# Strassen's scheme for feed-forward blocks 12 to 15 of the opening token group in place of blocks 16 to 19 of the middle group, with the weight sums of four parts made in two lists

## The chip, the core and the metric

The kernel runs on one core of a Trainium2 chip. The core has TensorE (matmuls, PE in the profile, its weight loads PEld), VectorE (DVE), ScalarE (ACT), GpSimd (POOL) and SyncE (SP, which here only issues transfers), and 16 DMA engines. The metric is the device time of one execution in microseconds, the median over several runs.

## What is computed

One layer of a hybrid encoder on 2048 prompt tokens and 64 sample tokens, model width 1024, all in float32: a modulated norm, one input projection, a pooling mixer beside a matrix-memory recurrence, an output projection; then the part that matters here, a gated feed-forward network of hidden width 2816 with a causal convolution of width 3:

```
h2 = rmsnorm(x, g2) * (1 + sc2) + sh2
up = h2 @ w_up                                  # 1024 -> 2 x 2816
conv = b_conv + sum(w_conv[j] * upp[:, j:j + T] for j in range(CONV_W))
a, g = jnp.split(conv, 2, -1)
x = x + gt2 * ((jax.nn.silu(g) * a) @ w_down)   # 2816 -> 1024
```

A final norm follows. The states of the recurrence, of the pool and of the convolution are returned as well.

## The kernel before, in words

**Precision.** Each matmul operand is split into a high and a low part (a ScalarE copy, line 427, and a VectorE subtraction, line 430, for a weight; the like for the moving side), and each product is three matmuls (`PASSES`, line 479). A matmul is 128 x 128 weights by up to 512 columns.

**Groups, blocks and parts.** The feed-forward works on the 2112 tokens in three groups of 704 (`fgroups`; below: opening, middle and last group). The hidden width is 22 blocks of 128. A group takes them in the parts that `PARTS` lists (line 33). In a part each block is first projected up (`Pair.products`, line 1709: Strassen's seven products, 12 matmuls of 352 columns each, so 84 a block; line 1604). Convolution, SiLU, gate and split of a block are spread over the products of the two blocks that follow (`step_2` to `step_7`, `scale_a`, `taps_a`, `gate` and others). The part's blocks are then projected down and added to the residual rows `x3` (`rows_add`, line 2038).

**Two down projections.** A *plain* part (`down`, line 2201) multiplies each block for 8 output rows and two column sections of 448 and 256: 48 matmuls a block, line 2212. A *Strassen* part, for which `paired` (line 38) is true, has four blocks and takes seven products in place of eight (`quad_down`, line 2045): 168 matmuls of 352 columns, line 2073, for the four. It runs one block late: the first block of the next part is projected up first. It needs its gated blocks as sums, made by `step_2` to `step_7` into seven buffers of the tag `av`, and weight sums. At its entry it waits for the last block's two sums from PSUM (`sum_g1`, `sum_a`, line 1613) before more banks are free. Before the change, Strassen parts are the middle group's first five and the last group's first four. The opening group is all plain, in parts of 5, 5, 6 and 6 blocks. The middle group ends with a plain part of two blocks, for which there is code of its own (`nf == 2`).

**Weight sums.** `quad_sums` (line 1654) makes them from `w_quad`, in pieces: a load of 512 KB, four VectorE operations, a store to `dsum` in DRAM. There are two indices `d` to a part and two pieces to an index. Its buffers are of the tag `av` too, which has seven (`AVB`). The weight sums of the up projection (`wsum`) are made earlier; in the opening group all seven units of a block are split, and three of them are stored with their split (`wsplit`), so that the later groups split four.

**Order of the work.** TensorE, ScalarE, VectorE and GpSimd run in the order in which the program is written. Weights come in one stream of units of up to 512 columns (`stream`), loaded by SP up to seven units ahead and split up to four ahead (`pump`, line 437). Work beside the stream is written as generators in the lists `bg[0]` and `bg[1]`. `tick(i)` takes one step of the first one in list `i`: a product has two steps of list 0, a block's products four of list 1, `quad_down` one of list 0 at each half product except that each fourth is one of list 1, `down` one for each row and block unless deferred work (`todo`) is due, of list 1 and 0 in turn. `drain(i)` runs a list to its end at once. List 0 has `quad_sums` in the opening group, and in the others first `final` (line 1915), the last norm of the group before with its stores. List 1 has `prepare` (norm and sums of the next group's inputs, stored to `Bd`), and in the last part `reload` (the seven inputs brought back as `hx`).

**The end of a group.** Before the last part is projected down, both lists are drained and `reload` is listed. After a plain part of six blocks, each finished row is squared by ScalarE and added up by GpSimd (`fsq_acc`, line 2028) as it ends. After the part of two blocks, `final` does this at the beginning of the next group, with VectorE for the additions (line 2034), and only six of the inputs are reloaded in the part, the seventh at the end.

Of the kernel before, what the change touches and what calls it, by code (L numbers as in the profile page):

```python
# [29 lines left out]
EB = 1  # L30
AVB = 7
ENDS = ((0, 448), (448, 704))
PARTS = (((0, 5), (5, 10), (10, 16), (16, 22)), ((0, 4), (4, 8), (8, 12), (12, 16), (16, 20), (20, 22)),
         ((0, 4), (4, 8), (8, 12), (12, 16), (16, 22)))
NQ, QUADS = 4, 5


def paired(g, part):
    return g > 0 and part[1] - part[0] == NQ
EPS = 1e-6  # L40
HD = 128
NH = 4
# [23 lines left out]
def tile_layer(ctx: ExitStack, tc: tile.TileContext, xT, vecs, cst, rst, w_mod, w_ada, w_qkou, w_v, w_pool,  # L66
# [38 lines left out]
    bg = ([], [], [], [], [])  # L105

    def tick(i=0):
        q = bg[i]
        while q:
            try:  # L110
                next(q[0])
                return
            except StopIteration:
                q.pop(0)

    def drain(*which):
        for i in which or (0, 1, 2, 3, 4):
            while bg[i]:
                tick(i)
# [153 lines left out]
    for g in range(NG):  # L273
        o = Grp()
# [83 lines left out]
    for g in range(NFG):  # L358
        held = None
        late = []  # L360
        for (f0, f1_) in PARTS[g]:
            for f in range(f0, f1_):
# [12 lines left out]
            for i, (n, k) in enumerate(order):  # L375
# [3 lines left out]
                if k % 4 == 0 or (n, c) not in seen:  # L379
                    seen.add((n, c))  # L380
                    d = min(c + 4, f1_)
# [287 lines left out]
    for g in range(NFG):  # L669
        o = Grp()  # L670
# [980 lines left out]

        act.activation(to.t[:, :FH], bk.t[:, :FH], AF.Copy)  # L1652

    def quad_sums():

        for d in range(2 * QUADS):
            for c in (0, 256):
                t = f2.tile([P, 2, FT], F32R, tag="av", name="qs", bufs=AVB)
                w = t.bitcast(F32).rearrange("p a t -> p (a t)")[:, :1024].rearrange("p (i c) -> p i c", i=4)
                nc.sync.dma_start(out=w, in_=w_quad[d, :, :, c:c + 256])  # L1660
                for _ in range(5):
                    yield
                a11, a12, a21, a22 = (w[:, i] for i in range(4))
                dve.tensor_tensor(out=a22, in0=a21, in1=a22, op=ALU.add)
                yield
                dve.tensor_tensor(out=a21, in0=a11, in1=a21, op=ALU.subtract)
                yield
                dve.tensor_tensor(out=a11, in0=a22, in1=a11, op=ALU.subtract)
                yield
                dve.tensor_tensor(out=a12, in0=a12, in1=a11, op=ALU.subtract)  # L1670
                yield
                yield
                nc.sync.dma_start(out=dsum[d, :, :, c:c + 256], in_=w)
                yield
                yield
                yield

# [20 lines left out]
    class Pair:  # L1698
# [3 lines left out]
        quad = d = None  # L1702
# [189 lines left out]
    def reload(Bo, names):  # L1892
        for nm in names:
            Bo.load(nm)
            yield
            yield

    def load_x2(o, ks=range(KD)):
        x3 = []
        for k in ks:  # L1900
            x = f2.tile([P, FT], F32, tag=f"x{k}", name=f"x{k}")
            nc.sync.dma_start(out=x, in_=x2d[k, :, o.t0:o.t0 + FT])
            x3.append(x)
        return x3
# [247 lines left out]
    for o in fgroups:  # L2152
        Bo = B[o.g]
        held = None
        for pi, part in enumerate(PARTS[o.g]):
            f0, f1_ = part
            nf = f1_ - f0
            lastp = pi == len(PARTS[o.g]) - 1
            ends = o.last and lastp
            av = [None] * nf  # L2160
            quad = Quad() if paired(o.g, part) else None
            if pi == 0:
                pair = None
            for f in range(f0, f1_):
                old, pair = pair, Pair(o, Bo, f, f - f0, av, quad)
                pair.products(old)
                if o.g == 0 and len(x3) < KD or pi == 0 and not bg[0]:
                    x3 += load_x2(o, range(len(x3), min(len(x3) + 2, KD)))
                if held is not None and nf > 2:
                    quad_down(o, held, pair, old)  # L2170
                    held = None
            if pi == 0 and o.g > 0:
                drain(0)
                x3 += load_x2(o, range(len(x3), KD))
            if not o.last:
                if pi == 0:
                    if o.g == 0:
                        bg[0].append(quad_sums())
                    bg[1].append(prepare(fgroups[o.g + 1], fscr))
                if lastp:  # L2180
                    drain(0, 1)
                    if nf == 2:
                        for p in (old, pair):
                            p.d = f1.tile([P, 2, HX], F32R, tag="hx", name="av", bufs=2 * len(BN))
                    B.append(Sums())
                    bg[1].append(reload(B[-1], ("B11", "T1", "T2", "B21", "B22", "T3") if nf == 2 else BN))
# [89 lines left out]
            pair = None  # L2276
        if not o.last:
            drain(1)
            if nf == 2:
                Bn = B[-1]  # L2280
                Bn.load(BN[-1])
            bg[0].append(final(o, x3, ssum, nf == 2))
            x3 = []
# [87 lines left out]
```

## Time and profile before

| | |
|---|---|
| median of three runs | 2170.43 us (2169.34 to 2173.03) |
| the profiled execution | 2169.81 us |
| its span, first to last instruction | 2168.0 us |
| granted TensorE clock, mean | 0.998 |
| VectorE, ScalarE, GpSimd busy | 77%, 51%, 12% |
| HBM read, written | 414.65 MB, 128.08 MB |
| DMA, mean rate over the span | 252 GB/s |

How to read the profile: busy rows give line, engine, operation, names (out<-in), shape and count, then busy us, mean ns of one, and the engine's idle time before them. The chain of work that ended last gives start and length in us of each piece. The timeline merges neighbours on one engine; a number in square brackets is idle time, with what ended it. Matmuls are pipelined, so the mean of one (over 300 ns) is longer than the distance from one start to the next, which is the pitch. Tables by stretch give the stretch, its length, busy time and count of each engine, the granted clock, the DMA engines' busy share and GB/s. By time, the feed-forward begins near 787 us; the middle group begins at 1251.6 us and the last at 1701.3 us.

### The profile page before, as it was taken

What the parts mean: (1) busy time and instruction counts of PE and PEld (TensorE: products, weight loads), DVE (VectorE), ACT (ScalarE), POOL (GpSimd) and SP (SyncE); (2) the same over time, 40 slices, a digit from 0 to 9 for tenths busy, and PEclk for the clock granted to TensorE, in tenths of its full rate; (3) what the DMA queues carried; (4) which work ended last, traced back from release to release, by engine and by line L of the source; (5) the groups of instructions that cost most, each with busy time, mean ns of one, the idle gap of its engine ahead of it and who ended that gap; (6) DMA issues with size and microseconds to landing.
All of it is one profiled execution on the core that took longest, in us unless ns stands there. A gap on an engine that the chain in (4) does not pass through costs nothing.

```text
span 2168.0 us, 38128 instructions
## 1 busy us (share of the span) xinstructions
PE 2146.5 (99%) x13529; PEld 2040.9 (94%) x13529; DVE 1666.4 (77%) x3107; ACT 1104.1 (51%) x2201; POOL 249.3 (12%) x468
## 2 busy tenths in 40 slices
PE   8999999999999999999999999999999999999998
PEld 7888888888899999999999999999999999999998
DVE  5777678677675878797968668988888797887874
ACT  4554335334333556464736445655656455565554
POOL 0010000001000301010101220100101121111112
PEclk9999999999999999999999999999999999999999
DMA  8987997897788686888968976666666875555542
GB/s 317 330 307 228 321 317 252 282 320 269 246 286 281 229 268 232 293 288 301 353 235 307 319 264 206 226 227 200 219 232 230 277 269 190 171 175 188 173 157 76
DMA packets 302439, 545.28 MB, mean 252 GB/s; under 512 B 25984, under 2 KB 118656, under 8 KB 302248
## 3 DMA queue, kind: packets, MB, share of 16 engines
q1 hardware_dynamic: 291656, 517.64, 70.6%
q10 hardware_dynamic: 10592, 25.20, 3.0%
q8 instruction: 107, 1.75, 0.3%
q14 instruction: 84, 0.69, 0.1%
HBM read 414.65 MB, written 128.08 MB: 250 GB/s over the span
## 4 chain that ended last, share of the span: by engine, by line
PE 60%; DVE 3%; DMA 1%; issue 1%; ACT 1%; POOL 0%; SPq 0%; DVEq 0%; POOLq 0%; ACTq 0%
PE mm L1604 37%; PE mm L2212 11%; PE mm L2073 10%; PE mm L494 2%; DVE wt L430 1%; DVE tg L1582 0%; ACT tg L1577 0%; DMA wt<-dsum 0%; DMA wt<-wsum 0%; DMA fscr<-h2d 0%; DVE ea L1613 0%; DVE eg L1613 0%; DVE x L2042 0%; DVE tg L1809 0%; ACT mm L1652 0%
## 5 line engine op out<-in xcount | busy, mean ns | idle before, releaser
L1604 PE MATMUL mm<-hx,wt 128*128 128x352 f32 x5544 | 887.1, 321 | 0.9 <-DVE wt L430 0.7
L1604 PEld LDWEIGHTS mm<-hx,wt 128*128 128x128 f32 x5544 | 880.5, 188 | 2.2 <-DVE wt L430 1.9
L494 PE MATMUL mm<-hl,wt 128*128 128x512 f32 (+2 forms) x1920 | 385.8, 356 | 0.3 <-DMA wt<-hl_kept 0.3
L427 ACT ACTIVATE wt<-raw 128x512 fp32r<-128x512 f32 (+3 forms) x468 | 275.9, 597 | 191.0 <-PE mm L494 53.4
L430 DVE TENSOR_TENSOR wt<-raw,wt 128x512 fp32r<-128x512 f32 (+3 forms) x468 | 307.3, 663 | 74.8 <-ACT wt L427 73.3
L494 PEld LDWEIGHTS mm<-hl,wt 128*128 128x128 f32 x1920 | 314.7, 188 | 48.1 <-issue 4.4
L2073 PE MATMUL mm<-av,wt 128*128 128x352 f32 x1512 | 248.2, 324 | 2.7 <-DVE ea L1613 1.2
L2073 PEld LDWEIGHTS mm<-av,wt 128*128 128x128 f32 x1512 | 242.3, 188 | 6.2 <-DVE ea L1613 4.0
L2042 DVE SCALAR_TENSOR_TENSOR x<-mm,MOD,x 128x352 f32<-128x352 f32 (+5 forms) x384 | 180.3, 508 | 69.0 <-PE mm L2212 54.1
L2212 PE MATMUL mm<-av,wt 128*128 128x448 f32 (+1 forms) x1440 | 232.2, 322 | 0.0
L2212 PEld LDWEIGHTS mm<-av,wt 128*128 128x128 f32 x1440 | 221.2, 188 | 9.9
L1652 ACT ACTIVATE mm<-mm 128x352 f32<-128x352 f32 x204 | 91.4, 448 | 235.9 <-PE mm L1604 176.6
L494 PE MATMUL mm<-mx,wt 128*128 128x512 f32 (+1 forms) x960 | 182.2, 351 | 1.2 <-DVE scr L266 1.2
L494 PEld LDWEIGHTS mm<-mx,wt 128*128 128x128 f32 x960 | 158.5, 188 | 24.1 <-DVE scr L266 1.1
L1582 DVE SCALAR_TENSOR_TENSOR ta<-ea,V,ta 128x704 f32<-128x704 f32 (+1 forms) x132 | 125.6, 952 | 54.8 <-ACT ta L1577 48.2
L1582 DVE SCALAR_TENSOR_TENSOR tg<-eg,V,tg 128x704 f32<-128x704 f32 (+1 forms) x132 | 125.7, 952 | 50.5 <-ACT tg L1577 48.0
L430 DVE TENSOR_TENSOR wt<-wt 128x512 fp32r<-128x512 f32 x204 | 138.4, 683 | 11.6 <-ACT wt L427 11.6
L427 ACT ACTIVATE wt<-wt 128x512 fp32r<-128x512 f32 x204 | 123.6, 622 | 34.0 <-DMA wt<-wsum 31.0
L1560 POOL COPY ea<-UC 128x2 f32<-128x2 f32 x66 | 32.7, 496 | 510.4 <-DVE ta L1582 429.1
L1801 ACT ACTIVATE tg<-tg 128x704 f32<-128x704 f32 (+1 forms) x66 | 52.4, 794 | 69.3 <-DVE tg L1582 69.3
L1143 PE MATMUL mm<-wt,hl 128*128 128x256 f32 (+1 forms) x576 | 71.2, 284 | 0.0
L1143 PEld LDWEIGHTS mm<-wt,hl 128*128 128x128 f32 x576 | 70.2, 189 | 0.8 <-issue 0.6
(306 smaller groups left out, 2220.2 us busy)
## 6 DMA issues: line engine op xcount, KB each, us to landing
wt<-wsplit SPq DMA_DIRECT2D x132, 512.0 KB, 4.3
raw<-w_up SPq DMA_DIRECT2D x198, 256.0 KB, 4.3
wt<-hl_kept SPq DMA_DIRECT2D x96, 512.0 KB, 6.3
wt<-wsum SPq DMA_DIRECT2D x132, 256.0 KB, 5.2
wsplit<-wt SPq DMA_DIRECT2D x66, 512.0 KB, 5.4
w<-w_up SPq DMA_DIRECT2D x88, 256.0 KB, 4.8
wsum<-w SPq DMA_DIRECT2D x44, 512.0 KB, 6.0
Bd<-fscr ACTq DMA_DIRECT2D x56, 352.0 KB, 4.4
```

Of the source, the lines that this page charges most:

```text
L427: act.activation(u.w[:, 0, :u.n], u.raw[:, :u.n], AF.Copy)
L430: dve.tensor_tensor(out=u.w[:, 1, :u.n], in0=u.raw[:, :u.n], in1=u.w[:, 0, :u.n].bitcast(F32), op=ALU.subtract)
L494: pe.matmul(ps[bi][:, :hi - lo], U[:, a, k % 4 * P:(k % 4 + 1) * P], mv[k][:, b, lo:hi], start=(at == 0 and pi == 0), stop=(k == order[-1] ...
L1143: pe.matmul(ps[ti][:n, :cols], h[4 * kh + k4][:, b, lo:lo + n], U[:, a, k4 % 2 * cols:(k4 % 2 + 1) * cols], start=(kh == 0 and k4 == 0 and ...
L1560: pool.tensor_copy(ext[:, 0:2], UC[:, f, :])
L1582: dve.scalar_tensor_tensor(out=t[:, :E], in0=ext[:, j:j + E], scalar=wc(j, f), in1=t[:, :E], op0=ALU.mult, op1=ALU.add)
L1604: pe.matmul(bk.t[:, :FH], U[:, a, kc * P:(kc + 1) * P], Bo.at(nm, kc, b), start=(first and kc == 0 and pi == 0), stop=(kc == 3 and pi == 2 ...
L1652: act.activation(to.t[:, :FH], bk.t[:, :FH], AF.Copy)
L1801: act.activation(self.tg[:, :E], self.tg[:, :E], AF.Silu)
L2042: dve.scalar_tensor_tensor(out=x3[n][:, a:b], in0=bk.t[:, a - lo:b - lo], scalar=gt2(n, s), in1=x3[n][:, a:b], op0=ALU.mult, op1=ALU.add)
L2073: pe.matmul(bk.t[:, :FH], U[:, a, c:c + P], quad.put(op, m, b), start=(first and m == 0 and pi == 0), stop=(m == 1 and pi == 2), skip_grou ...
L2212: pe.matmul(bks[i].t[:, :hi - lo], U[:, a, k % 4 * P:(k % 4 + 1) * P], av[k][:, b, lo:hi], start=(k == 0 and (a, b) == PASSES[0]), stop=(k ...
```

## The change

The opening group's parts become 6, 6, 4 and 6 blocks, the third (12 to 15) by Strassen's scheme. The middle group's last parts (16 to 19 and 20 to 21) become one plain part of six, as in the last group. So there are four Strassen parts' weight sums to make and not five, in two lists: the first, for the part of blocks 12 to 15 and the indices 0 to 2, is listed where the only one was; the second is listed right after the new Strassen part. The first must be complete before block 12, and a drain is put there; the second is drained at the end of the opening group. One of the 13 steps of a piece goes. With the part of two blocks gone, the branches for `nf == 2` are not taken any more.

```diff
-PARTS = (((0, 5), (5, 10), (10, 16), (16, 22)), ((0, 4), (4, 8), (8, 12), (12, 16), (16, 20), (20, 22)),
+PARTS = (((0, 6), (6, 12), (12, 16), (16, 22)), ((0, 4), (4, 8), (8, 12), (12, 16), (16, 22)),
          ((0, 4), (4, 8), (8, 12), (12, 16), (16, 22)))
-NQ, QUADS = 4, 5
+NQ, QUADS = 4, 4
+SUMS = ((6, 7, 0, 1, 2), (3, 4, 5))
...
 def paired(g, part):
-    return g > 0 and part[1] - part[0] == NQ
+    return part[1] - part[0] == NQ
...
-    def quad_sums():
+    def quad_sums(ds):
 
-        for d in range(2 * QUADS):
+        for d in ds:
             for c in (0, 256):
...
                 nc.sync.dma_start(out=dsum[d, :, :, c:c + 256], in_=w)
-                yield
                 yield
                 yield
...
             quad = Quad() if paired(o.g, part) else None
+            if quad is not None and o.g == 0:
+                drain(0)
...
                     quad_down(o, held, pair, old)
                     held = None
+                    if o.g == 0:
+                        bg[0].append(quad_sums(SUMS[1]))
...
                     if o.g == 0:
-                        bg[0].append(quad_sums())
+                        bg[0].append(quad_sums(SUMS[0]))
                     bg[1].append(prepare(fgroups[o.g + 1], fscr))
                 if lastp:
-                    drain(0, 1)
+                    drain(1) if o.g == 0 else drain(0, 1)
...
         if not o.last:
             drain(1)
+            if o.g == 0:
+                drain(0)
             if nf == 2:
```

## The prediction

> **What bounds the kernel now.** I read the page first, then the chain of work that ended last, then TensorE's timeline at the places that the change touches, and last the busy time of the engines by stretch.
>
> ```profile
> PE 2146.5 (99%) x13529; PEld 2040.9 (94%) x13529; DVE 1666.4 (77%) x3107; ACT 1104.1 (51%) x2201; POOL 249.3 (12%) x468
> ```
>
> TensorE (PE) is busy for 99% of the span, so a change matters only through the number of matmuls, through their pitch, or through the few waits between them. The chain in the feed-forward part shows both forms of the down projection:
>
> ```profile
> 1126.13 77.90 PE mm L1604 x492
> ...
> 1209.81 41.99 PE mm L2212 x264
> ...
> 1399.54 4.02 PE mm L2073 x24
> ...
> 1405.46 23.06 PE mm L2073 x144
> ```
>
> Line 1604 is the up projection, 84 matmuls for one hidden block: 77.90 / 492 = 158.3 ns each, 13.3 us a block. Line 2212 is the plain down projection, 48 matmuls a block (159.1 ns), line 2073 Strassen's, 168 for four blocks (160.1 ns). Nothing but TensorE stands in these rows: the stages run at its pitch, and other engines show only at the seams.
>
> **The change part by part.** *Matmuls.* The opening group loses 4 plain blocks (192 matmuls of line 2212) and gains one Strassen part (168 of line 2073); the middle group does the reverse. Each scheme's count over the program stays (1440 and 1512), so this term is 0. One part is worth 192 x 159.1 - 168 x 160.1 = 3.7 us, which the opening group gains and the middle one gives back. What remains are seams.
>
> *The seam from the middle to the last group* now stands behind a part of two blocks. After the change it is built as the seam from the opening to the middle group is now: a six-block plain part, the seven reloads inside its down projection, squares added on GpSimd as the rows finish. So the two seams of the same trace are compared, the good one first:
>
> ```profile
> 1263.19 55.26 PE L1604 MATMUL mm<-hx,wt 128*128 128x352 f32 x348
> 1318.29 0.32 PE L735 MATMUL m<-fscr,ones_r 128*128 128x352 f32 x1
> ...
> 1318.93 4.35 PE L2073 MATMUL mm<-av,wt 128*128 128x352 f32 x24
> 1323.12 2.06 PE L1604 MATMUL mm<-hx,wt 128*128 128x352 f32 x12
> ```
>
> ```profile
> 1701.27 11.89 PE L1604 MATMUL mm<-hx,wt 128*128 128x352 f32 x74
> 1713.88 4.71 PE L1604 MATMUL mm<-hx,wt 128*128 128x352 f32 x28 [0.72 <-DVE wt L430]
> 1718.43 1.38 PE L1924 MATMUL m<-ones_r,ssum 128*128 128x1 f32 x12
> ...
> 1725.39 45.73 PE L1604 MATMUL mm<-hx,wt 128*128 128x352 f32 x276
> 1770.96 3.05 PE L2073 MATMUL mm<-av,wt 128*128 128x352 f32 x18
> ...
> 1775.46 2.06 PE L1604 MATMUL mm<-hx,wt 128*128 128x352 f32 x12
> ```
>
> From start to start: 348 matmuls take 55.10 us in the good seam, 158.3 ns each. In the bad one 102 take 17.16 us where 16.15 are due (1.0 us lost, most of it a wait for a weight split, L430); 276 take 45.57 where 43.70 are due (1.9 lost); the first 24 of Strassen's take 4.50 against 4.19 (0.3 lost). VectorE is late there because it adds the squares itself, which it no longer does after the change:
>
> ```profile
> L2034 DVE TENSOR_TENSOR ssum<-ssum,fscr 128x704 f32<-128x704 f32 x7 | 6.2, 891 | 3.9 <-ACT fscr L2033 3.5
> ```
>
> The 1.9 us are no wait but a slower pitch, as this stretch shows, 134 matmuls in 22.00 us (164 ns) with the granted clock at 1.00 (the third number from the end):
>
> ```profile
> 1728.00:1750.00 22.00, 22.00 (x134) 22.00 (x133) 21.00 (x37) 12.69 (x23) 7.02 (x14) 1.00 0.90 319
> ```
>
> It begins at this seam and not at the good one, so I count it as the seam's; its bounds are 0 (it returns elsewhere) and 1.9, and I take 1.9, the row of the seam that the new one copies. (The Trainium skill, page "TensorE: Matmul & The Clock Gate", section "Back-to-back issue gap", gives one warm pitch, columns / 2.4 GHz + 2.5 ns, an estimate of 149 ns for 352 columns. No row here has it: 158 and 164 ns stand at the same clock, so the measurement decides. By that rule there is no second pitch for the seam to set off, this term is nothing, and the sum would be 0.1 us slower instead of 1.8 faster.)
>
> *The Strassen part that goes* was the middle group's fifth:
>
> ```profile
> 1656.55 4.34 PE L2073 MATMUL mm<-av,wt 128*128 128x352 f32 x24
> 1660.73 2.07 PE L1604 MATMUL mm<-hx,wt 128*128 128x352 f32 x12
> ```
>
> Its first 24 take 4.18 us where 24 x 160.1 = 3.84 are due: 0.3 us of entry wait go. Together 1.0 + 1.9 + 0.3 + 0.3 = 3.5 us go.
>
> *The Strassen part that comes*, in the opening group, has an entry too, which the trace doesn't show there. The nearest rows are the middle group's, its second part in the chain above (23.06 us for the 144 inside, 4.02 for the first 24) and its third in the timeline:
>
> ```profile
> 1479.87 3.05 PE L2073 MATMUL mm<-av,wt 128*128 128x352 f32 x18
> 1483.68 1.23 PE L2073 MATMUL mm<-av,wt 128*128 128x352 f32 x6 [0.77 <-DVE ea L1613]
> 1484.74 2.06 PE L1604 MATMUL mm<-hx,wt 128*128 128x352 f32 x12
> 1486.64 8.81 PE L2073 MATMUL mm<-av,wt 128*128 128x352 f32 x54
> 1496.18 14.68 PE L2073 MATMUL mm<-av,wt 128*128 128x352 f32 x90 [0.72 <-DVE x L2042]
> 1510.69 4.60 PE L1604 MATMUL mm<-hx,wt 128*128 128x352 f32 x28
> ```
>
> The second loses 4.02 - 3.84 = 0.2 us; the third 4.87 - 3.84 = 1.0 at its entry and 24.05 - 23.06 = 1.0 inside. Bounds 0.2 and 2.0. I take 1.0, the entry of the third: the new part has more splits on VectorE ahead of the sums (L1613) that free its banks.
>
> *VectorE around the new part.* The opening group splits all seven weight units of a block, the later ones four. The busy time of line 430 alone, then of all engines (the columns are TensorE, weight load, VectorE, ScalarE, GpSimd):
>
> ```profile
> 1126.00:1204.00 78.00, 27.11 (x41) 1.00 0.92 320
> 1348.00:1399.00 51.00, 10.87 (x16) 1.00 0.65 231
> ```
>
> ```profile
> 1000.00:1078.00 78.00, 78.00 (x495) 77.96 (x495) 69.45 (x116) 53.89 (x98) 11.69 (x20) 1.00 0.99 346
> 1348.00:1399.00 51.00, 51.00 (x324) 51.00 (x323) 41.97 (x66) 32.95 (x60) 6.12 (x14) 1.00 0.65 231
> 1318.00:1348.00 30.00, 29.93 (x187) 29.64 (x187) 28.11 (x52) 16.69 (x34) 1.31 (x2) 1.00 0.58 185
> ```
>
> A block in front of Strassen's part, with the next group's inputs prepared beside it, costs VectorE 41.97 x 13.3 / 51 = 10.9 us in the middle group. In the opening group come (27.11 / 78 - 10.87 / 51) x 13.3 = 1.8 us of splits: 12.7 of 13.3 us, 96%. This applies to blocks 14, 15 and 16, where the products' sums of the gated blocks are due. VectorE reached 95% once with TensorE fully busy (21.00 of 22.00, above), otherwise 89% beside products (69.45 of 78) and 94% beside Strassen's (28.11 of 30). At 95% the three blocks lose nothing; at 89% they last 14.3 us, 3 x 1.0 = 3.0 lost. Bounds 0 and 3.0; I take 0.7, near the 95% row, as weights are split up to four units (four products of 1.9 us) ahead.
>
> *The weight sums* move from one list of 20 pieces to one of 10 and one of 6:
>
> ```profile
> L1664 DVE TENSOR_TENSOR qs<-qs x20: 407/419/423, 877.3 to 1180.0; 128x256 f32<-128x256 f32 x20
> ...
> DMA to landing us min/median/max: 3.5/6.2/9.6
> ```
>
> Four pieces go: 16 VectorE operations of 0.42 us (6.7 us) and 8 transfers on SP's queue, all beside busy TensorE, so I cost them at 0. The first list must end before block 12. It needs 10 x 12 = 120 steps; the code offers 20 in a six-block down projection (its 48 steps are shared with the other list and with deferred work), 14 a block in six blocks, less 2 that stand in the next down projection's 20, and those 20: 122. So the new drain ahead of block 12 finds nothing. The second list needs 72, and blocks 17 to 21 with the down projection offer 88; its drain finds nothing either, and one list's loads stay out of the new part's own transfers.
>
> *Sum.* -3.5 + 1.0 + 0.7 = -1.8 us. The profiled run of 2169.81 us (its span 2168.0) becomes 2168.0; the median of the runs shown lies 0.62 above that run, so I forecast **2168.6 us**. With the bounds: from 3.3 faster (-3.5 + 0.2) to 3.4 slower (-1.6 + 2.0 + 3.0), 2167.1 to 2173.8.
>
> **The rivals.** (1) *Given back:* VectorE in the opening group costs what the seam saves: entry 2.0 and 1.5 in the blocks, 0.0 in sum, 2170.4. For it: 96% of VectorE's time is spoken for. Against it: the 95% row.
> (2) *Slower, VectorE becomes the bound.* It decides if VectorE can't pass 89% beside products from block 12 on. Then five blocks lose 1.0 each, the part itself 28.11 / 0.89 - 30 = 1.6, and the entry costs 2.0: 8.6 - 3.5 = 5.1 slower, 2175.5. Against it: the same 95% row, and 94% in every Strassen part.
> (3) *Faster by more:* the middle group's third part, with its 2.0 us of stalls, meets other work beside it and loses them, and the new entry costs 0.2: -3.3 - 2.0 = -5.3, 2165.1. For it: the second part has the same code and 0.2. Against it: nothing of that part is edited.
> (4) *It doesn't do what it says:* the first list isn't done, and the drain puts a last piece's 6.2 us of landing and 4 x 0.42 of operations in front of VectorE's work: 7.9 us, less three units split ahead (3 x 1.9), 2.2 lost: 2170.8.
>
> **How the numbers follow.** Forecast 0.45, (1) 0.25, (2) 0.10, (3) 0.13, (4) 0.07. The range for 8 in 10 takes in the bounds, half of (3), and stops short of (2): 2165.0 to 2174.5. About 0.2% (4.3 us) is what a measurement of this kernel can tell from no change. Faster by that, under 2166.1: case (3) and the forecast's best tail, 0.15. Slower, over 2174.8: case (2), and 0.03 from (1) and (4), 0.13. Within: 0.72.
>
> **What would show it.** Right: lines 1604, 2073 and 2212 keep their counts; the seam into the last group has no wait for a weight split and a pitch of 158 ns; the new part's first 24 matmuls take 4.0 to 4.9 us; no operation of the sums stands bunched ahead of block 12. Wrong: waits of TensorE for splits in blocks 14 to 16, or a stretch of pitch over 160 ns behind the new part, which could last as long as this one and more; either takes the gain away. A stall over 2 us at the new entry, or VectorE under 90% with TensorE waiting for it, is rival (2).

## The result, and the profile after

The changed kernel takes **2178.33 us** (median of six runs, 2175.40 to 2182.43), the kernel before 2170.76 (six runs); the ratio is 1.0035, 95% interval 1.0022 to 1.0048. It is slower by some 7.6 us, where 2168.6 was forecast and 2165.0 to 2174.5 was the range. The profiled execution took 2179.77 us with a span of 2178.0, 10.0 us over the span before. The edits shift the lines: 1604 is now 1605, 2212 is 2216, 430 is 431, 1613 is 1614; 2042 and 2073 keep their numbers.

```profile
PE 2151.7 (99%) x13529; PEld 2045.1 (94%) x13529; DVE 1649.5 (76%) x3060; ACT 1103.5 (51%) x2193; POOL 263.3 (12%) x475
```

The count of matmuls is the same, VectorE has 47 operations fewer, GpSimd seven more. So the page alone shows no cause: TensorE's busy time grew by 5.2 us with the same matmuls (a slower pitch counts as busy), and the rest of the 10.0 us is waiting.

To find the place I took the distance from each matmul's start to the next and subtracted the usual pitch: 158.3 ns for 352 columns, 199.7 for 448, 119.3 for 256. What is left is the loss, in us, here by stage (the new part's column holds also the 12 matmuls of line 1605 inside its entry):

| | blocks 0-5 | 6-11 | 12-16 | new part | 17-21 | opening group | middle | last | feed-forward begins |
|---|---|---|---|---|---|---|---|---|---|
| before | 0.7 | 0.5 | 0.2 | - | 0.0 | 1.6 | 6.2 | 7.4 | 787.2 |
| after | 0.7 | 3.4 | 2.4 | 5.3 | 3.4 | 15.2 | 4.5 | 4.0 | 788.7 |

Opening group +13.6, middle -1.7, last -3.4, and 1.5 from the part ahead, whose code is the same (in the 15 runs below the feed-forward begins between 786.3 and 792.2 us): 10.0 of the 10.0. Nothing of the change runs there: the record of the granted clock of after has 0.50 for 3.4 us from 750.6 us, as have 8 of the 15 runs near that time, and the record of before has not. The last two groups gave 5.1 us, where 3.5 were forecast. The opening group lost 13.6, in four places.

**The seam into the last group**, TensorE's timeline of after:

```profile
1714.67 4.91 PE L1605 MATMUL mm<-hx,wt 128*128 128x352 f32 x30
...
1726.23 55.26 PE L1605 MATMUL mm<-hx,wt 128*128 128x352 f32 x348
1781.33 4.39 PE L2073 MATMUL mm<-av,wt 128*128 128x352 f32 x24
```

348 matmuls from 1726.23 to 1781.33, 158.3 ns each: no bracket with a wait, no slow stretch. The good seam was copied as planned.

**Blocks 6 to 11**, the second part of the opening group, the same view:

```profile
917.24 38.48 PE L1605 MATMUL mm<-hx,wt 128*128 128x352 f32 x242
957.05 13.57 PE L1605 MATMUL mm<-hx,wt 128*128 128x352 f32 x84 [1.34 <-DVE wt L431]
971.51 23.09 PE L1605 MATMUL mm<-hx,wt 128*128 128x352 f32 x144 [0.88 <-DVE wt L431]
994.90 3.76 PE L1605 MATMUL mm<-hx,wt 128*128 128x352 f32 x22 [0.30 <-DVE wt L431]
998.49 1.76 PE L2216 MATMUL mm<-av,wt 128*128 128x448 f32 x9
```

492 matmuls in 81.25 us where 77.9 are due; TensorE waits three times for a weight split. The busy time by stretch (VectorE is the third busy column), first of after, then of before:

```profile
917.00:955.00 38.00, 38.00 (x243) 38.00 (x242) 27.01 (x46) 22.16 (x41) 3.42 (x7) 1.00 0.97 342
955.00:998.00 43.00, 40.48 (x252) 39.62 (x251) 42.36 (x71) 31.45 (x56) 7.71 (x13) 1.00 0.99 347
```

```profile
1000.00:1038.00 38.00, 38.00 (x242) 38.00 (x242) 30.92 (x54) 24.76 (x46) 4.25 (x8) 1.00 0.96 336
1038.00:1078.00 40.00, 40.00 (x255) 39.96 (x254) 38.53 (x63) 29.13 (x53) 7.44 (x12) 1.00 1.02 356
927.00:960.00 33.00, 32.88 (x207) 32.56 (x206) 32.24 (x53) 25.89 (x47) 5.16 (x10) 1.00 0.97 347
```

VectorE has 71% of the first half and 98.5% of the second. Before, the stretch that the prediction read as 89% over 78 us was 81% and then 96%: the mean hid a second half with almost nothing free. The share alone doesn't say what is lost: the third row of before, in another part, has 97.7%, and TensorE is busy there for 32.88 of 33.00 us. One wait of VectorE itself is new, in the view of the sums' tile of after (before has no such row):

```profile
its engine sat idle before it (us, times) until:
  DMA qs<-w_quad: 1.9, 2
```

**Blocks 12 to 16 and the entry of the new part:**

```profile
1099.93 13.49 PE L1605 MATMUL mm<-hx,wt 128*128 128x352 f32 x82 [1.67 <-DVE wt L431]
1113.26 0.49 PE L2073 MATMUL mm<-av,wt 128*128 128x352 f32 x2
1114.38 2.83 PE L2073 MATMUL mm<-av,wt 128*128 128x352 f32 x16 [0.63 <-DVE wt L431]
1119.56 2.13 PE L2073 MATMUL mm<-av,wt 128*128 128x352 f32 x6 [2.34 <-DVE ea L1614]
1121.49 2.64 PE L1605 MATMUL mm<-hx,wt 128*128 128x352 f32 x12
1123.96 3.21 PE L2073 MATMUL mm<-av,wt 128*128 128x352 f32 x19
```

The first 24 take 8.23 us (1113.26 to 1121.49) where 3.84 are due, the next 12 take 2.47 for 1.90. The two waits hold 2.97 us of it. Most of the rest is the clock, the third number from the end in this stretch:

```profile
1113.00:1124.00 11.00, 8.02 (x40) 7.43 (x39) 10.93 (x21) 5.89 (x11) 1.53 (x3) 0.84 0.65 211
```

The record of the granted clock has 0.50 for 3.4 us from 1119.3; the matmuls there stand 292 to 294 ns apart. VectorE is busy for 10.93 of 11.00 us. What it does ahead of the sum that frees the banks (line 1614):

```profile
1112.65 0.52 DVE L785 TENSOR_TENSOR fscr<-fscr 128x352 fp32r<-128x352 f32 x1
1113.20 0.53 DVE L781 TENSOR_TENSOR fscr<-fscr 128x352 f32<-128x352 f32 x1
...
1114.85 0.52 DVE L785 TENSOR_TENSOR fscr<-fscr 128x352 fp32r<-128x352 f32 x1
1115.29 0.95 DVE L781 TENSOR_TENSOR fscr<-fscr 128x352 f32<-128x352 f32 x2
...
1118.99 0.52 DVE L1614 TENSOR_TENSOR ea<-mm,s 128x352 f32<-128x352 f32 x1
```

Lines 781 and 785 are the middle group's preparation: five operations, 2.5 us, ahead of the sum that TensorE waits 2.34 us for.

**Behind the new part**, one row for blocks 17 to 21:

```profile
1147.01 68.14 PE L1605 MATMUL mm<-hx,wt 128*128 128x352 f32 x408
1214.99 3.24 PE L2216 MATMUL mm<-av,wt 128*128 128x448 f32 x19
```

408 matmuls in 67.98 us, 166.6 ns, where 64.6 us are due. The row has no bracket, the granted clock is 1.00. Start by start the pitch is 158.3 ns until 1158.79, there is one distance of 430 ns and one of 268, and then 333 matmuls stand 166 to 167 ns apart until the plain down projection.

### The profile page after: what moved, and what is told of

Its sections match the earlier page's. It is cut to its first block, busy times and chain, and to the rows that moved or that the text cites. A ratio compares the mean times of both kernels' runs of the same rounds, so it can differ in the third digit from the quotient of the medians.

```text
span 2178.0 us, 38048 instructions
## 1 busy us (share of the span) xinstructions
PE 2151.7 (99%) x13529; PEld 2045.1 (94%) x13529; DVE 1649.5 (76%) x3060; ACT 1103.5 (51%) x2193; POOL 263.3 (12%) x475
## 4 chain that ended last, share of the span: by engine, by line
PE 57%; DVE 4%; DMA 2%; issue 1%; ACT 1%; SPq 0%; POOL 0%; DVEq 0%; ACTq 0%; POOLq 0%
PE mm L1605 35%; PE mm L2216 10%; PE mm L2073 9%; PE mm L495 2%; DVE wt L431 1%; DVE tg L1583 1%; DMA wt<-dsum 1%; DMA wt<-wsum 0%; ACT tg L1578 0%; DVE x L2042 0%; DMA fscr<-h2d 0%; DVE eg L1614 0%; DVE fscr L748 0%; DMA raw<-w_up 0%; DVE ea L1614 0%
## 5 line engine op out<-in xcount | busy, mean ns | idle before, releaser
L431 DVE TENSOR_TENSOR wt<-raw,wt 128x512 fp32r<-128x512 f32 (+1 forms) x460 | 310.4, 680 | 80.6 <-ACT wt L428 79.1
L428 ACT ACTIVATE wt<-raw 128x512 fp32r<-128x512 f32 (+1 forms) x460 | 274.5, 604 | 167.6 <-PE mm L495 56.1
L2042 DVE SCALAR_TENSOR_TENSOR x<-mm,MOD,x 128x352 f32<-128x352 f32 (+3 forms) x368 | 171.3, 505 | 73.9 <-PE mm L2216 58.7
```

Source lines behind the costliest of these rows:

```text
L428: act.activation(u.w[:, 0, :u.n], u.raw[:, :u.n], AF.Copy)
L431: dve.tensor_tensor(out=u.w[:, 1, :u.n], in0=u.raw[:, :u.n], in1=u.w[:, 0, :u.n].bitcast(F32), op=ALU.subtract)
L2042: dve.scalar_tensor_tensor(out=x3[n][:, a:b], in0=bk.t[:, a - lo:b - lo], scalar=gt2(n, s), in1=x3[n][:, a:b], op0=ALU.mult, op1=ALU.add)
```

## The experiments

The kernel before ran beside each set of runs: 2172.14 us in the median with the first four, 2172.49 with e5 to e8, 2171.80 with e9 to e12, 2173.77 with e13 to e15. Ratios are to it, and are not quotients of these medians. Losses by stage of each profiled execution, as above:

| | 0-5 | 6-11 | 12-16 | new part | 17-21 | last down, rest | middle | last | median us | ratio, 95% |
|---|---|---|---|---|---|---|---|---|---|---|
| e1_after_again | 0.7 | 3.4 | 2.2 | 5.3 | 3.4 | 0.1 | 4.5 | 4.1 | 2180.18 | 1.0037 (1.0025-1.0048) |
| e2_seam_only | 0.1 | 0.1 | 0.2 | - | 0.0 | 0.3 | 5.5 | 4.1 | 2172.52 | 1.0004 (0.9995-1.0014) |
| e3_prep_early | 0.7 | 10.8 | 0.1 | 0.5 | 0.6 | 2.5 | 4.9 | 4.0 | 2182.81 | 1.0054 (1.0036-1.0073) |
| e4_sums_early | 0.7 | 1.9 | 3.0 | 5.3 | 0.6 | 0.1 | 4.8 | 4.0 | 2176.10 | 1.0018 (1.0009-1.0027) |
| e5_narrow | 0.7 | 4.3 | 2.9 | 4.9 | 0.8 | 0.0 | 4.4 | 4.0 | 2177.97 | 1.0031 (1.0019-1.0044) |
| e6_prep_from_0 | 0.4 | 2.9 | 0.1 | 0.5 | 0.6 | -0.2 | 5.9 | 4.4 | 2171.08 | 0.9994 (0.9985-1.0003) |
| e7_both_from_0 | 2.1 | 1.7 | 0.1 | 0.5 | 0.6 | -0.3 | 4.4 | 4.6 | 2172.08 | 0.9998 (0.9989-1.0007) |
| e8_paced | 0.4 | 0.2 | 0.1 | 0.5 | 0.6 | 13.4 | 4.5 | 4.5 | 2183.88 | 1.0056 (1.0043-1.0069) |
| e9_spread | 0.8 | 0.7 | 0.1 | 0.5 | 3.4 | -0.3 | 4.7 | 4.0 | 2170.34 | 0.9994 (0.9985-1.0003) |
| e10_spread_6 | 0.3 | 0.7 | 0.1 | 0.5 | 3.4 | -0.3 | 5.0 | 4.2 | 2170.62 | 0.9994 (0.9985-1.0003) |
| e11_second_list | 0.8 | 0.8 | 0.1 | 0.5 | 1.8 | 4.1 | 11.5 | 4.1 | 2179.27 | 1.0030 (1.0018-1.0042) |
| e12_narrow_all | 0.5 | 4.8 | 3.0 | 4.6 | 3.5 | 0.0 | 5.6 | 5.4 | 2187.12 | 1.0068 (1.0054-1.0082) |
| e13_late | 0.1 | 5.0 | 2.9 | 4.4 | 0.2 | 0.1 | 5.0 | 4.0 | 2179.80 | 1.0029 (1.0017-1.0041) |
| e14_spread_late | 0.8 | 0.7 | 0.1 | 0.5 | 0.2 | -0.3 | 4.7 | 4.0 | 2169.11 | 0.9984 (0.9975-0.9993) |
| e15_no_ops | 0.7 | 0.1 | 2.2 | 3.5 | 0.6 | 0.1 | 4.5 | 4.4 | 2176.55 | 1.0012 (1.0001-1.0024) |

The **theory** from these two profiles: VectorE has no room beside the opening group's products when the weight sums and the next group's preparation stand there together, and late splits and sums hold TensorE. The **rivals**: the time is an accident of one execution; the seam didn't pay; the transfers, not VectorE, are late.

### The change again, and its seam alone

> The changed kernel once more. Its first profile lost, against its matmuls at 158.3 ns: 3.4 us in blocks 6 to 11 (waits for weight splits), 2.4 us in blocks 12 to 16, 5.0 us at the entry of the new Strassen part, and 3.4 us in blocks 17 to 21 at a pitch of 167 ns. Theory A (VectorE is crowded around the new part): the waits and the entry return at the same blocks, within 1 us. Theory B (a short wait of TensorE sets off the slow pitch, by chance): the slow stretch need not return, and the time moves by 3 us from run to run. Rival C (the losses are disturbance of one execution): they don't return. A and B: 2175 to 2180 us; C: near 2171.

The four losses come back within 0.3 us each, and the slow stretch has 333 matmuls again. It is no accident.

In e2 the opening group stays plain and the middle one ends with the part of six:

```diff
-PARTS = (((0, 6), (6, 12), (12, 16), (16, 22)), ...
+PARTS = (((0, 5), (5, 10), (10, 16), (16, 22)), ...
-SUMS = ((6, 7, 0, 1, 2), (3, 4, 5))
+SUMS = (tuple(range(8)), ())
...
```

(The parts left out put the 13th step of a piece and the drain of both lists back as they were.)

> One half of the change alone: the middle group ends with a plain part of six, the opening group stays all plain in parts of 5, 5, 6, 6; eight Strassen parts in place of nine, the sums of four parts in one list. One Strassen part fewer costs 192 x 159.1 - 168 x 160.1 = 3.7 us. If the seam is worth what the two profiles show (3.5 us), the time is that of before, +0.2 us. If the seam's gain is a chance of the slow pitch in one execution (1.9 of the 3.5), +2 us. If the middle group's end has nothing to do with the gain, +3.7 us.

The last group loses 4.1 us in place of 7.4 and the total is that of before: the missing Strassen part's 3.7 us is about what the seam gives. The time alone does not exclude the second branch (+2 us), since the interval reaches up to 3.0 us. The profiles speak for the first: in none of the 16 with the new seam does a slow stretch stand behind it. But the old seam was profiled once, so whether its slow stretch, 1.9 of the 3.5 us, comes in each execution is not shown.

### VectorE's work in blocks 6 to 11

e4 begins the first list at block 0, with six more empty steps a piece (18 in place of 12):

```diff
-                for _ in range(5):
+                for _ in range(5 + more):
...
+                if o.g == 0:
+                    bg[0].append(quad_sums(SUMS[0], 6))
...
-                    if o.g == 0:
-                        bg[0].append(quad_sums(SUMS[0]))
```

> The changed kernel, with the first list of weight sums begun at block 0 and spread over 18 steps a piece (6 more between load and first operation) in place of 12. Theory S (the sums' operations, packed into blocks 6 to 11 beside the preparation, and a load that VectorE waits 1.7 us for, cause the waits there): the 3.4 us lost in blocks 6 to 11 go, and the rest stays: 3 to 4 us faster than the changed kernel. Rival (the waits there are from the preparation and the splits): blocks 6 to 11 still lose over 2 us.

It takes 4.1 us off the changed kernel that ran beside it (2180.18 to 2176.10), about what theory S forecast, but not for its reason. Blocks 6 to 11 fall from 3.4 to 1.9 only, between the two forecasts, and 2.8 us come from the slow stretch behind the new part, which is gone with no edit there. So e4 decides nothing about these blocks.

e15 leaves the first list's four operations out, and keeps its transfers:

```diff
-                dve.tensor_tensor(out=a22, in0=a21, in1=a22, op=ALU.add)
+                if ds != SUMS[0]:
+                    dve.tensor_tensor(out=a22, in0=a21, in1=a22, op=ALU.add)
...
```

> The changed kernel without the four VectorE operations of each piece of the first list; the loads and the stores stay, so the sums of the weights concerned are replaced by the weights' own quarters. It tells the time of VectorE, with its waits for the loads, from the transfers. Theory A (VectorE): blocks 6 to 11 lose under 1 us in place of 3.4, the entry of the new part and blocks 12 to 16 keep their 5 to 7.5 us since the preparation is still beside them; the time is 2 to 4 us under the changed kernel, 2175 to 2177. Theory B (the 20 transfers of the list in these blocks slow the weights): blocks 6 to 11 still lose 2.5 us or more.

Blocks 6 to 11 lose 0.1 us, and the time, 2176.55, is in the forecast of theory A. Stretches of e15:

```profile
917.00:955.00 38.00, 38.00 (x245) 38.00 (x244) 23.43 (x35) 22.16 (x42) 3.45 (x8) 1.00 0.87 288
955.00:998.00 43.00, 43.00 (x273) 42.79 (x272) 40.24 (x62) 33.44 (x60) 7.35 (x13) 1.00 1.01 371
```

TensorE is busy throughout while the DMA engines are as full as in after in the second half, where the waits stood (1.01 and 371 GB/s, against 0.99 and 347), so the transfers are not the cause: the operations, with VectorE's waits for their loads, are. The two were not told apart, since both go here. The entry still loses 3.5 us, as expected: it has another cause.

### The preparation at the entry

e6 lists the preparation at block 0 in place of behind the first part's products:

```diff
             if pi == 0:
                 pair = None
+                if o.g == 0:
+                    bg[1].append(prepare(fgroups[1], fscr))
...
-                    bg[1].append(prepare(fgroups[o.g + 1], fscr))
+                    if o.g > 0:
+                        bg[1].append(prepare(fgroups[o.g + 1], fscr))
```

> The middle group's preparation in the opening group is listed from block 0 on in place of behind the first part's products, so that 88 of its 91 steps are done by block 12; the weight sums stay as in the changed kernel. Theory A (VectorE's work, crowded ahead of the new part, makes the waits at its entry, and these waits let the granted clock fall): the entry of the new part loses under 1 us for its first 36 matmuls in place of 4.4 to 5.0, blocks 12 to 16 under 0.5 in place of 2.4 to 3.2, the granted clock stays 1.00 in the stretch of the entry, and with no short wait behind it the slow pitch of blocks 17 to 21 is gone or begins elsewhere. Blocks 6 to 11 still lose 3 us or somewhat more, since the sums still begin there and VectorE has only part of the preparation less. Total 6 to 9 us under the changed kernel: 2169 to 2173 beside 2171 before. Theory B (the entry is late for another reason, its own sums from PSUM or the weights' transfers): the entry keeps 3 us and more, and the total stays over 2175. Theory C (work is only moved, as when the extra steps stood in the plain down projections): the entry is clean, blocks 0 to 11 lose as much as the entry gains, total 2177 to 2181.

This one list, begun earlier, takes the kernel from a ratio of 1.0037 (e1) to 0.9994, as theory A forecast. Blocks 12 to 16 fall from 2.4 to 0.1 and the new part from 5.3 to 0.5; the slow stretch (2.8 us) is gone as well, with no edit there. TensorE's timeline of e6 at the entry:

```profile
1112.66 4.20 PE L2073 MATMUL mm<-av,wt 128*128 128x352 f32 x24
1116.69 2.06 PE L1605 MATMUL mm<-hx,wt 128*128 128x352 f32 x12
1118.59 23.21 PE L2073 MATMUL mm<-av,wt 128*128 128x352 f32 x144
```

The first 24 take 4.03 us, no wait over the view's threshold, and the clock stays at 1.00. VectorE has no more room than in after, by stretch (it is the third busy column):

```profile
1105.00:1116.00 11.00, 11.00 (x70) 10.80 (x69) 10.60 (x17) 9.10 (x18) 1.28 (x3) 1.00 0.83 289
1116.00:1127.00 11.00, 11.00 (x71) 11.00 (x70) 11.00 (x21) 6.14 (x13) 1.01 (x2) 1.00 0.56 162
```

It is busy for 21.60 of 22.00 us, and TensorE for all of them. What changed is which operations stand ahead of the sums that TensorE needs, not how full VectorE is. Blocks 6 to 11 keep 2.9 us: their loss is the sums', this one the preparation's.

e3 had tried the same with extra steps of the preparation inside the first two plain down projections:

```diff
                         tick(1 - c // len(secs) % 2)
+                        if o.g == 0 and pi < 2 and c // len(secs) % 2:
+                            tick(1)
```

> The changed kernel, with 18 more steps of the preparation list in each of the first two plain down projections, where VectorE is idle a third of the time: the preparation of the next group ends before block 12 instead of inside the new part's entry. Theory A1 (the preparation's steps stand ahead of the sums that the entry waits for, five of them, 2.6 us): the entry of the new part falls from 5.0 us lost to under 1.5, the granted clock stays at 1.00 there, and blocks 12 to 16 lose under 1 us of their 2.4: 4 to 6 us faster than the changed kernel. Rival A2 (seven weight splits a block alone crowd VectorE): entry still loses over 3 us, and the time stays within 2 us of the changed kernel.

The entry is as clean (0.5), but blocks 6 to 11 lose 10.8, and the total misses its forecast. VectorE is not the bound there (36.10 of 43.00 us busy between 955 and 998). Its waits and SP's between 917 and 1000, of e3:

```profile
DVE qs L1665 <- DMA qs<-w_quad: 6.5, 4, 3.0
DVE wt L431 <- ACT wt L428: 4.3, 3, 3.5
```

```profile
SPq L415 <- DMA wsplit<-wt: 14.2, 5, 6.5
SPq L436 <- DVE wt L431: 9.2, 6, 3.7
SPq L1674 <- DVE qs L1671: 7.9, 4, 3.8
```

VectorE waits 6.5 us for the sums' loads, and SP, whose queue holds those loads, waits for VectorE's sums and splits. I read this as a ring: engines that run in the order of the program wait for each other. No run isolates it, and SP's waits for VectorE don't show it by themselves: in e14, below, it waits 32.7 us for splits in the same stretch, and blocks 6 to 11 lose 0.7. What is shown is that a theory of VectorE's time alone is too narrow: where a step stands counts as well as how long it is.

e7 has both lists from block 0 on, the sums with 18 steps a piece:

> Both the preparation and the first list of weight sums begin at block 0, the sums with 18 steps a piece in place of 12. If VectorE's load by stretch sets the losses, spreading both over 12 blocks is best of all: blocks 6 to 11 lose under 1.5 us, blocks 12 to 16 under 0.5, the entry under 1, total 8 to 12 us under the changed kernel, 2167 to 2170. If list buffers or transfers set them (a part of six blocks leaves one free buffer for the sums), blocks 6 to 11 still lose 3 us or the first part begins to lose, and the total is 2171 to 2176.

The second branch: the first part begins to lose (2.1 us), blocks 6 to 11 still lose 1.7, and the time is that of before. To spread evenly is not enough.

### The slow pitch

e5 puts a matmul of 128 columns ahead of blocks 17 to 21, e12 ahead of every block but block 0 of each group (the edit shown is e5's):

```diff
             b1 = self.b1 = take()
+            if o.g == 0 and f > 16:
+                pe.matmul(b1.t[:, :128], ones_r, Bo.at("B11", 0, 0)[:, :128], start=True, stop=True)
```

> One matmul of 128 columns, whose result is overwritten, stands ahead of each of blocks 17 to 21 of the opening group; everything else is the changed kernel. It tests the stretch of 333 matmuls at 166 to 167 ns each between 1159 and 1215 us, which costs 2.7 to 3.4 us at a granted clock of 1.00. Theory A: the slow pitch is a relation between the weight loads and the matmuls that a short wait sets and that any break in the even row of 352-column matmuls resets: the stretch ends at the first of the five new matmuls behind it, within 84 matmuls, and the loss of blocks 17 to 21 falls from 3.4 us to under 1.5; the five matmuls themselves cost about 0.3 us; the time is about 2 us under the changed kernel's, near 2178. Theory B: it belongs to what runs beside it (the same transfers, the same buffers) and lasts until those change: the stretch keeps its 300 matmuls and more, the time is the changed kernel's or 0.3 us above. The losses of blocks 6 to 11 (3.0 to 3.5 us) and of the entry (4.4 to 5.0) are as in the changed kernel under both.

> The changed kernel with a matmul of 128 columns ahead of every block of the feed-forward except block 0 of each group (63 in all, about 0.06 us each, 3.6 us together). In e5_narrow such matmuls stood ahead of blocks 17 to 21 and the slow stretch did not begin there, but another of 163 matmuls stood in blocks 9 to 11, where none was. If a matmul of another width ends the slow pitch, no stretch of it here is longer than one block (84 matmuls). If it does not, stretches of 160 matmuls and more remain. The losses at waits for weight splits and at the new entry stay as in the changed kernel (opening group 11 to 14 us); total about that of the changed kernel plus 0 to 3 us, 2178 to 2183.

In e5 the loss and the time are those of theory A, but the stretch was not cut short: it did not begin in blocks 17 to 21, and one of 163 matmuls stood in blocks 9 to 11, after a break of some 1.1 us and until the plain down projection. e12 decides against theory A: its stretch from 1158 to 1218 us has 347 matmuls and runs through four of the narrow ones. A matmul of another width doesn't end it. The losses at the waits stayed, as forecast; the time is 4 us above the forecast's end. The profile shows why: a narrow matmul takes 56 to 59 ns to the next start, and that next one 212 to 217 ns in place of 158. So each costs 0.11 us and not 0.06, and 63 of them make 7.1 us, about the 7.0 us by which the span (2185.0) is longer than that of after.

e13 takes away the operations that stand where it begins, by 12 empty steps ahead of the second list; e14 does so to e9, below:

```diff
+        for _ in range(lead):
+            yield
...
-                        bg[0].append(quad_sums(SUMS[1]))
+                        bg[0].append(quad_sums(SUMS[1], lead=12))
```

> The changed kernel with 12 empty steps ahead of the second list of weight sums, which moves its first operations on VectorE from block 17 into block 18. In the runs so far a slow stretch of 330 to 347 matmuls behind the new part began in every case right at a wait of TensorE of 0.1 to 0.3 us for a weight split at the end of block 17, just where the first three operations of the list (0.42 us each) stand between the splits. Theory A (these operations make the wait, and the wait sets the slow pitch): the wait and the stretch are gone, blocks 17 to 21 lose under 1 us in place of 3.4, the time is 2.5 to 3.4 us under the changed kernel: 2175 to 2176. Theory B (the wait has another source, or another wait takes its place): the wait and the stretch remain within two blocks, and the time is that of the changed kernel, 2177 to 2180. The losses of blocks 6 to 16 and of the entry are untouched.

The wait of 0.4 us at the end of block 17 and the stretch are gone in both (blocks 17 to 21 lose 0.2). But e13's time is not measurably better than the changed kernel's and lies where theory B put it: its profile has 165 slow matmuls from 974 to 1002, in code that is the same. So with no wait there no stretch began, but which waits begin one stays open: in e3, e4, e6, e7, e8 and e15 the same break at the same place (429 to 435 ns from start to start, against 426 to 437 in after, e1, e9 and e10) left the pitch at 158.

### A better order

e8 paces: preparation from block 0; three indices of sums only in the first two down projections (a list of its own, 16 steps a piece); five behind the new part, with an extra step at each event of the last down projection:

```diff
-SUMS = ((6, 7, 0, 1, 2), (3, 4, 5))
+SUMS = ((6, 7, 0), (1, 2, 3, 4, 5))
...
+                        bg[4].append(quad_sums(SUMS[0], 4))
...
                         tick(1 - c // len(secs) % 2)
+                    if o.g == 0:
+                        tick(4 if pi < 2 else 0)
```

> The preparation begins at block 0; the first list holds only the three indices that the new part needs first and its steps stand only in the first two down projections, where VectorE has the most room (down projections split fewer weights), 16 steps a piece; the second list holds five indices and gets one step more at each event of the opening group's last down projection. If VectorE's crowding beside the up projections is all that the change costs, the opening group loses about 2 us in place of 15, the seam's gain stays, and the total is 2164 to 2168, below both the kernel before and the changed one. If the later list makes the stretch behind the new part lose instead (five indices in blocks 17 to 21 and their down projection), the opening group loses 5 us or more behind 1148 us and the total is 2169 to 2173.

All 22 blocks and the new part lose 1.8 us together, about what the first branch has, but the last down projection loses 13.4, and the total is over that of both branches. VectorE's wait in the sums' tile of e8:

```profile
  DMA qs<-w_quad: 21.8, 6
```

TensorE waits twice there for weight splits (5.33 and 3.88 us) that stand behind such waits, and the granted clock is 0.50 for 6.8 and 3.4 us beside them. With two steps an event, a piece's operations stand too close behind its load; that was the first reading. e11 gives that list one index less and 14 steps a piece:

> As e9_spread, but index 2 stands in the second list (four indices, 14 steps a piece, with one step of list 0 more at each event of the last down projection). If the short distance from load to operation was the cause of the 13.6 us in e8_paced, the last down projection loses under 2 us here and the total is that of e9_spread within 2; if any sums in that down projection hold up its weights, it loses 5 us or more.

It falls between the branches: 4.1 us in that down projection, 13.8 us of VectorE's waits for loads, and 7 more in the middle group, 4.5 of them in its block 0 and some 2.8 in a slow stretch of 347 matmuls. The queue shows what the distance in steps did not mend: in e8 a load is issued at 1241.38, when VectorE has already waited for it since 1235.7. SP waits 10.2 us (in e11 5.7) in that down projection to issue such loads until the store of the piece before has landed, because six gated blocks leave one of the seven `av` buffers. Both versions that put more sums there lost by it, so the next ones put none more there. e9 leaves the second list at three indices and puts one in blocks 0 to 5 and one in 6 to 11, 36 steps a piece; e10 puts both in blocks 6 to 11, 20 steps a piece:

```diff
+            if o.g == 0 and pi < 2:
+                bg[0].append(quad_sums((1 + pi,), 24))
```

> Preparation from block 0; three indices of weight sums paced in the first two down projections as in the run e8_paced, one index in blocks 0 to 5 and one in blocks 6 to 11 (36 steps a piece), the last three behind the new part as in the changed kernel. e8_paced lost 0.0 to 0.7 us in any block up to 21 and 13.6 us in the last down projection, where VectorE waited 21.8 us for the sums' loads. If those two findings are all there is, the opening group loses 1 to 3 us in place of 15, the seam's gain stays (last group 4.0 to 4.6), and the total is 4 to 7 us under the kernel before: ratio 0.9968 to 0.9982. If two more indices in the blocks crowd VectorE again, the opening group loses 4 to 6 and the ratio is 0.9985 to 1.0000.

> As e9_spread, but both indices (four pieces of 20 steps) stand in blocks 6 to 11. If VectorE's load there decides, these blocks lose 1 to 2 us more than in e9_spread and the total is 1 to 2 us higher; if the pace of a piece decides (12 steps in the changed kernel, 20 here), they lose under 0.5 and the two kernels are equal.

They are equal, as the pace branch has it (0.7 us in blocks 6 to 11 in both, where under 0.5 was forecast). The ratio of e9 and the opening group's 5.2 us are those of its second branch, but not for its reason: blocks 0 to 11 lose 1.5 us. What is missing is one thing, the slow stretch of 330 to 333 matmuls from 1150 us on. e14 is e9 with the 12 empty steps:

> The kernel of e9_spread with the same 12 empty steps ahead of the second list. e9_spread lost 5.2 us in the opening group, 3.4 of them in a slow stretch from 1150 to 1206 us. Theory A: the stretch is gone, the opening group loses 1.5 to 2.2 us and the total is 3 us under e9_spread: ratio to the kernel before 0.9975 to 0.9985, faster than both kernels. Theory B: the stretch stays, ratio 0.9990 to 0.9998.

TensorE's timeline of e14:

```profile
1107.74 4.19 PE L2075 MATMUL mm<-av,wt 128*128 128x352 f32 x24
1111.77 2.06 PE L1605 MATMUL mm<-hx,wt 128*128 128x352 f32 x12
1113.67 23.21 PE L2075 MATMUL mm<-av,wt 128*128 128x352 f32 x144
1136.72 64.98 PE L1605 MATMUL mm<-hx,wt 128*128 128x352 f32 x408
1201.54 4.03 PE L2223 MATMUL mm<-av,wt 128*128 128x448 f32 x24
```

The opening group loses 2.0 us, the 408 matmuls behind the new part take 64.82, and the time is 2169.11: ratio 0.9984 (0.9975 to 0.9993), 0.16% or about 3.5 us under the kernel before, and the only version whose interval lies below it. Its gain over e9 rests on the profile (3.4 us to 0.2 in blocks 17 to 21): the two ran in different sets, and their intervals overlap.

## Why the prediction was wrong, point by point

- **Matmuls, 0:** right, 13529 in both.
- **The seam, -3.2, and the part that goes, -0.3:** right. The last group loses 3.4 less. The middle one loses 1.7 less, more than the 0.3; its third part met less waiting as well (1.6 in place of 2.3 us), a piece of rival (3).
- **The entry of the new part, +1.0, bounds 0.2 to 2.0: this step failed.** It measured 5.0 (4.4 in the first 24 matmuls, 0.6 in the next 12). The rows were the middle group's, where VectorE has 82% of the stretch ahead; here the preparation's operations stood ahead of the sums that free the banks, and the waits brought half a clock with them. e6 moves the preparation and the entry costs 0.2, with VectorE as full. The upper end of the bounds was two stalls of a quieter group, not what late sums behind other work can do.
- **Blocks 14 to 16, +0.7, bounds 0 to 3.0:** the place was right and the size low: 2.4 us in blocks 12 to 16, inside the bounds, 2.2 of them in block 15. They go with the preparation too (0.1 in e6).
- **The weight sums, 0: failed too.** "All beside busy TensorE" looked at TensorE, and the cover had to be looked for on VectorE, which had 98%, 96% and 87% before in the second halves of the opening group's second, third and fourth part. Blocks 6 to 11 lose 3.4 us, and 0.1 without the operations. That the drain ahead of block 12 finds nothing was right: the list's last store is issued at 1036.3, block 12 begins at 1046.3.
- **The slow pitch:** the seam's 1.9 us went as counted, and the text's own warning, a stretch of over 160 ns behind the new part, cost 3.4 and stood in no sum. The lower bound of that term, 0 because it returns elsewhere, was the nearer one: more came back than went. What makes it return stays open.
- **The rivals:** (2) has the sign and nearly the price (5.1 against 7.6), and its mark, a stall over 2 us at the entry. Its condition was wrong: VectorE passes 89% with ease (98.5%), and TensorE waits all the same. What decides is not a ceiling under 100% but a queue: in order, an operation that TensorE needs stands behind some that nobody needs yet. The nearness of its price is luck: its five blocks were priced at 5.0 us and lost 2.4, the inside of the part at 1.6 and lost nothing (23.05 us for the 144), the entry at 2.0 and lost 5.0, and the 6.8 us of blocks 6 to 11 and 17 to 21 stand in none of its terms.

Four terms of the opening group, 3.4 + 2.4 + 5.0 + 3.4 = 14.2 us, stand where the sum had 1.7.

## What to carry to other kernels

Before costing side work at nothing, cut the stretch that covers it into halves and read the engine that does the work, not the one that is to be hidden behind. If it is nearly full, ask which operation that the bound engine needs will stand behind the new work: with VectorE at 97.7% TensorE stood idle for 0.1 us in one stretch here, with 98.5% for 2.5 in another, and at the entry of e6 for nothing with VectorE just as full. When a stage moves into a busier group, its entry is priced from that group's engines, and the lists of side work have to be spread again: here that was worth 0.5% or some 11 us (ratio 1.0035 to 0.9984), where the prediction gave the move itself 1.8. Check the spread for the buffers too: with one of them free, the load of a piece waited here for the store of the piece before.

## What was not expected of the hardware

TensorE has two lasting pitches for the same matmul at a granted clock of 1.00, 158.3 and 166.7 ns. The second begins at a break in the even row, mostly a wait of 0.1 to 1.8 us, is not ended by single matmuls of 128 columns (e12), and holds until another break or other matmuls, up to 347 matmuls here. What decides whether a break sets it was not found: the same one set it in four profiles and not in six.

The granted clock fell to 0.50 for 3.4 us after waits of 0.63 and 2.34 us with 16 matmuls between (after, at 1119.3). In e15 it did not at the same place:

```profile
1111.36 2.83 PE L2077 MATMUL mm<-av,wt 128*128 128x352 f32 x16 [0.32 <-DVE wt L431]
1116.52 1.23 PE L2077 MATMUL mm<-av,wt 128*128 128x352 f32 x6 [2.33 <-DVE ea L1614]
1117.59 2.06 PE L1605 MATMUL mm<-hx,wt 128*128 128x352 f32 x12
1119.49 7.69 PE L2077 MATMUL mm<-av,wt 128*128 128x352 f32 x47
```

The 12 matmuls behind the same wait take 1.90 us, 158 ns each. (The Trainium skill, page "TensorE: Matmul & The Clock Gate", section "What's actually happening", has the clock halved after at least one idle window of about 3.4 us and restored after as long a busy one. The 3.4 us of half clock agree; the longest single wait ahead of them was 2.34 us.)
